# Sixteen modulation pieces moved between three stages, and gate products over the whole array, in a two-block model on one core

## The chip, the cores and the metric

The kernel runs on one core of a Trainium2 chip. The metric is the device time of one execution in microseconds. The kernel before was run three times: median 3736.88 us, lowest 3733.0, highest 3741.73. One more execution was recorded by the hardware profiler; it took 3748.67 us, and its span, the time between the first and the last recorded event, is 3746.9 us. All rows below are from that execution, counted from the span's start.

Five engines work side by side, each through its own list of instructions in order: PE (matrix products), DVE and POOL (elementwise), ACT (functions, copies) and SP, which here only issues DMAs. Nearly all DMAs of the kernel are issued by SP and share one hardware queue.

## The reference, cut to what matters

Two blocks run one after the other on 512 tokens of width 1024, in f32. The change lies in the first. Its layer 0 mixes by Fourier transforms, its layer 1 is an RWKV layer; both end in a mixture of 16 experts.

```python
for i in range(DEPTH):                       # first block, two layers
    sh1x, sc1x, g1x, sh2x, sc2x, g2x = split(silu(c) @ ada_w[i] + ada_b[i], 6)   # modulation, and so for ctx
    hx = rmsnorm(x, norm_g[i, 0]) * (1.0 + sc1x) + sh1x
    if i % 2 == 0: x = x + g1x * fourier_mix(hx, ...)
    else:                                    # RWKV, for x and ctx together 768 rows
        xr, xw, xk, xv, xa, xg = [h + (h_shift - h) * mix[j] for j in range(6)]
        r, k, v = xr @ wr, xk @ wk, xv @ wv
        decay[d] = f(w0[d] + tanh(xw @ w1[d]) @ w2[d])     # low rank, two directions d
        a[d] = sigmoid(a0[d] + (xa @ a1[d]) @ a2[d])       # low rank
        ...                                  # scan over time, output
    hx = rmsnorm(x, norm_g[i, 1]) * (1.0 + sc2x) + sh2x
    x = x + g2x * ec_moe(hx, ...)            # per expert the top 64 tokens (ctx: 32) and their gates
```

The product `silu(c) @ ada_w[1]` makes 6144 numbers for x and as many for ctx. Its first 8 of 24 pieces of 256 columns are made early; the other 16, the late pieces (n from 8 to 23), are needed only after the RWKV layer's projections.

## The kernel before, in words

**The RWKV layer's projections** run in this order on PE. First three low-rank products on mixed inputs (`lps`, L1193), while DVE and POOL make the mixed inputs (`c_mix`, L1085). Then r (eight blocks of 128 output columns, 512 tokens each), then v (eight blocks, 768 tokens), then the keys (eight blocks, 768 tokens). A block of these is made of products `pj` (L929 to L931): each f32 factor is split in a high and a low part, and three products make one. The split weights of a block come through one raw buffer `wraw` (load L913), an ACT cast to `whi` and a subtraction to `wlo` (L893, L894).

**The late modulation pieces** stand in the generator `modulation` (L1110). One piece is two half-pieces; each loads 512 KB (`adw`, L1119) and issues products of 32 columns of the array side by side (`mods`, L1128). After the second half ACT copies the result (`adasb`), and two small products (`mod2`, L1139) turn it. In the kernel before two half-pieces run ahead of the first `lps`, and all the others are placed between the products of r and v, by `beside=mods` in the function `big`, one step for every second index k.

**The key stage.** For each block m, `k_ahead(m)` (L1245) loads its small weights `w2`, `w0` and `a2` and the stored r and v (`rm`, `vm`), makes the decay logits `zps` (L1264), the rates `aps` (L1270) and cumulated decays `cps` (L1277). `k_evac(m)` takes the finished keys, makes their squared norm (`kn`, L1303), its inverse root `rn`, spreads it (`rnb`, L1315), multiplies (`kk`, L1317), and makes the tiles `bkt`, `art` (L1331 to L1339) and the bonus `bon` (L1353) that goes to `vm` (L1354). The tiles go to memory by stores (`keep`, L1283 to L1290), and `vm` by the store at L1356. A scheduler puts the instructions of each engine in order by its own estimates; what is in the code's text one behind the other can stand interleaved in the lists. On SP the order of the loads and stores is fixed by this too.

**The gates of the experts.** For each four experts, q from 0 to 3, `places(q)` makes matrices `Pm` of zeros and ones (L586), and `gates(q)` (L589) multiplies them by stored values to get each chosen token's number and gate. In each it uses products with 64 columns (L595) and, with ctx (layer 0), 32 columns (L599) of the array; DVE copies the sums out (L602 to L605), and a gather by POOL (L610) reads the chosen rows.

## Time and profile before

| what | value |
|---|---|
| median of three runs | 3736.88 us |
| profiled execution, and its span | 3748.67 us, 3746.9 us |
| PE busy | 3497.8 us (93% of the span) |
| DVE, ACT, POOL busy | 1745.7, 1134.1, 548.8 us (47%, 30%, 15%) |
| mean granted TensorE clock | 0.947 of full speed |

A busy time is the union of an engine's instructions. The whole span is dense on PE, so the reader asks for each stretch what PE waits for there, and not which engine is busiest on the whole. The stages in which the change works take 29.2 us (low-rank products), 149.8 us (r and v) and 207.4 us (keys) of the span.

### The profile page before, as it was taken

The numbers are of one execution on the slowest core, as the hardware profiler recorded it, in microseconds if no ns is written. First come the engines' busy times: TensorE is split into PE (matmuls) and PEld (weight loads), VectorE is DVE, ScalarE is ACT, GpSimd is POOL, SyncE is SP. The second block draws the span as 40 slices with busy tenths as digits, with TensorE's granted clock in tenths as the row PEclk, the third lists the DMA queues.
The fourth block names the chain that finished last, engine by engine and source line by source line (L and its number), as shares of the span: only waits on it lengthen the run. The fifth ranks groups of instructions, "written<-read, shape, count | busy, mean of one in ns | idle before, by whom it ended". The sixth has DMA issues, their size and how long they took to land. (4 is left out here: it accounts for less than half of the span.)

```text
span 3746.9 us, 64431 instructions
## 1 busy us (share of the span) xinstructions
PE 3497.8 (93%) x27320; PEld 2202.8 (59%) x27320; DVE 1745.7 (47%) x3279; ACT 1134.1 (30%) x2018; POOL 548.8 (15%) x458
## 2 busy tenths in 40 slices
PE   7989999997998688898999999999999989999999
PEld 4643333334787578886433335656788746567887
DVE  4522223228345578863112127845544558454443
ACT  3211110116446455532000004433322234242222
POOL 3100000002112233311000002220111222201111
PEclk9989999998998779998999998999999979999999
DMA  8489898852846757646999991111333321113332
GB/s 292 169 310 369 344 363 335 342 217 90 243 124 165 168 123 166 141 123 259 380 408 394 393 350 54 35 41 30 104 96 96 93 57 40 36 39 103 97 97 81
DMA packets 585941, 690.21 MB, mean 184 GB/s; under 512 B 178921, under 2 KB 454207, under 8 KB 585142
## 3 DMA queue, kind: packets, MB, share of 16 engines
q1 hardware_dynamic: 574192, 664.44, 52.7%
q10 hardware_dynamic: 8934, 13.12, 1.0%
q0 software_dynamic: 2528, 8.53, 0.6%
q8 instruction: 215, 3.52, 0.4%
q14 instruction: 72, 0.59, 0.0%
HBM read 646.17 MB, written 39.85 MB: 183 GB/s over the span
## 5 line engine op out<-in xcount | busy, mean ns | idle before, releaser
L893 ACT CAST whi<-wraw 128x1024 fp32r<-128x1024 f32 (+3 forms) x236 | 233.3, 989 | 684.7 <-PE pj L930 107.9
L640 PE MATMUL GU<-we,Xe 128*32 128x512 f32 x2048 | 306.0, 601 | 3.4 <-DVE hid L645 3.4
L894 DVE TENSOR_TENSOR wlo<-wraw,whi 128x1024 fp32r<-128x1024 f32 (+3 forms) x196 | 232.1, 1184 | 79.4 <-ACT whi L893 79.3
L665 PE MATMUL Y<-we,hidT 128*32 128x512 f32 x2048 | 262.1, 597 | 5.0 <-DVE Zc L697 3.5
L640 PE MATMUL GU<-we,Xq 128*32 128x512 f32 x2048 | 251.3, 610 | 0.0
L645 DVE TENSOR_TENSOR hid<-hid,GU 64x1536 f32<-64x1536 f32 (+1 forms) x32 | 47.7, 1491 | 360.0 <-ACT hid L644 359.9
L640 PE MATMUL GU<-we,Xc 128*32 128x512 f32 x1024 | 190.0, 597 | 0.0
L644 ACT ACTIVATE hid<-GU 64x1536 f32<-64x1536 f32 (+1 forms) x32 | 39.3, 1229 | 459.4 <-PE GU L640 459.3
L1985 POOL TENSOR_TENSOR u<-u 128x512 f32<-128x512 f32 x64 | 94.2, 1474 | 530.7 <-ACT uph L1984 530.7
L640 PEld LDWEIGHTS GU<-we,Xe 128*32 128x32 f32 x2048 | 79.0, 111 | 151.7 <-issue 145.9
L640 PEld LDWEIGHTS GU<-we,Xq 128*32 128x32 f32 x2048 | 67.6, 113 | 160.2 <-issue 157.7
L929 PE MATMUL pj<-hTh,whi 128*128 128x512 f32 (+1 forms) x352 | 155.5, 442 | 4.1 <-ACT hTh L1015 2.8
L665 PEld LDWEIGHTS Y<-we,hidT 128*32 128x32 f32 x2048 | 70.0, 110 | 148.9 <-issue 145.1
L931 PE MATMUL pj<-hTh,wlo 128*128 128x512 f32 (+1 forms) x352 | 149.6, 425 | 0.0
L930 PE MATMUL pj<-hTl,whi 128*128 128x512 f32 (+1 forms) x352 | 148.8, 423 | 0.0
L894 POOL TENSOR_TENSOR wlo<-wraw,whi 128x1024 fp32r<-128x1024 f32 x40 | 96.1, 2403 | 309.3 <-ACT whi L893 286.5
L654 DVE COPY hidT<-htp 128x512 f32<-128x512 f32 (+1 forms) x48 | 27.6, 600 | 209.7 <-PE htp L653 121.7
L929 PE MATMUL pj<-xh,whi 128*128 128x512 f32 (+1 forms) x320 | 120.6, 377 | 0.4 <-ACT xh L893 0.4
L710 DVE SCALAR_TENSOR_TENSOR xres<-sps,mod,xres 128x512 f32<-128x512 f32 x128 | 89.1, 746 | 64.9 <-PE sps L709 64.3
L930 PE MATMUL pj<-xl,whi 128*128 128x512 f32 (+1 forms) x320 | 115.0, 360 | 0.4 <-DVE xl L894 0.2
L931 PE MATMUL pj<-xh,wlo 128*128 128x512 f32 (+1 forms) x320 | 115.0, 359 | 0.0
L2152 ACT COPY PT<-tp 128x256 f32<-128x256 f32 (+3 forms) x128 | 51.2, 405 | 149.6 <-PE tp L2150 149.4
(2160 smaller groups left out, 7853.0 us busy)
## 6 DMA issues: line engine op xcount, KB each, us to landing
we<-in_moe_wd_dram SPq DMA_DIRECT2D x128, 1024.0 KB
we<-in_moe_wg_dram SPq DMA_DIRECT2D x126, 1024.0 KB
we<-in_moe_wu_dram SPq DMA_DIRECT2D x126, 1024.0 KB
ada<-in_ada_w_dram SPq DMA_DIRECT2D x32, 1024.0 KB
wraw<-in_w_up_dram SPq DMA_DIRECT2D x64, 512.0 KB
wraw<-in_w_down_dram SPq DMA_DIRECT2D x64, 512.0 KB
wraw<-in_w_in_dram SPq DMA_DIRECT2D x42, 512.0 KB
adw<-in_ada_w_dram SPq DMA_DIRECT2D x32, 512.0 KB
```

Of the source, the lines that this page charges most:

```text
L640: nc.tensor.matmul(GU[j:j + 32, g, :], xs[g][:, kk, :], ws[m][:, k, h * 512:(h + 1) * 512], start=kk == 0, stop=kk == 7, tile_position=(0, j))
L644: nc.scalar.activation(hid[up], GU[lo], AF.Silu)
L645: nc.vector.tensor_tensor(hid[up], hid[up], GU[up], ALU.mult)
L665: nc.tensor.matmul(Y[j:j + 32, 0, :], hidT[:, g, k, 32 * kh:32 * kh + 32], w[:, kh, h * 512:(h + 1) * 512], start=kh + k == 0, stop=kh * k ...
L710: nc.vector.scalar_tensor_tensor(r_[:, c, :], ps, g2[:, c, s:s + 1], r_[:, c, :], op0=ALU.mult, op1=ALU.add)
L893: e.nc.scalar.copy(hi, src)
L894: (eng or e.nc.vector).tensor_tensor(lo, src, hi, ALU.subtract)
L929: nc.tensor.matmul(ps, a[0], b[0], start=start, stop=False)
L930: nc.tensor.matmul(ps, a[0], b[1], start=False, stop=False)
L931: nc.tensor.matmul(ps, a[1], b[0], start=False, stop=stop)
L1985: nc.gpsimd.tensor_tensor(u, u, u, ALU.mult)
L2152: nc.scalar.copy(PT[:, :nb], tp[:, :nb])
```

## The change

Three things are changed.

First, the gates: products over the whole array. `Pm` is stored so that two experts' 64 columns, or four experts' 32, lie side by side as one matrix of 128 columns, and each product takes the values of all of them; the sums that belong to other experts are left unread. Per q there are 8 products where there were 16, and with ctx 2 where there were 8. DVE copies out by halves or quarters of the partitions: with ctx 8 copies instead of 4, without ctx 2 instead of 1.

Second, the 16 late pieces. Pieces 8 to 13 stand beside the mixing and the low-rank products, pieces 14 to 23 beside the key products; none stands beside r or v. The ACT copy of a piece is made in two halves.

Third, the buffers of the key stage: `w2` and `a2` have one buffer instead of two, and `sq` and `ks` share one.

```diff
         def gates(q):
-            pz = pm.tile([P, 3, 2], F32, name="pz", tag="m")
-            for i in range(4):
-                o = 64 * (i % 2)
+            pz = pm.tile([P, 3, 4, 2], F32, name="pz", tag="m")
+            es = lambda a, n_: V[:, t, 4 * q + a:4 * q + a + n_, :]
+            for j in range(2):
                 for t in range(4):
-                    nc.tensor.matmul(pz[o:o + 64, i // 2, :], Pm[:, t, i, :], V[:, t, 4 * q + i, :], start=t == 0, stop=t == 3,
-                                     tile_position=(0, o))
...
+                    nc.tensor.matmul(pz[:, j, 0:2, :], Pm[:, t, 2 * j:2 * j + 2, :].rearrange("p a b -> p (a b)"), es(2 * j, 2), start=t == 0, stop=t == 3)
             if with_ctx:
...
+                for t in (4, 5):
+                    nc.tensor.matmul(pz[:, 2], Pc[:, t - 4].rearrange("p a b -> p (a b)"), es(0, 4), start=t == 4, stop=t == 5)
+                for i in range(4):
+                    r = slice(32 * i, 32 * i + 32)
+                    nc.vector.tensor_copy(zc[r, q, :], pz[r, 2, i, :])
+                nc.vector.tensor_copy(ic[:, q:q + 1], zc[:, q, 0:1])
+            for h in range(2):
+                r = slice(64 * h, 64 * h + 64)
+                nc.vector.tensor_copy(zx[r, 2 * q:2 * q + 2, :], pz[r, 0:2, h, :])
+            if with_ctx:
+                nc.vector.tensor_copy(ix[:, 2 * q:2 * q + 2], zx[:, 2 * q:2 * q + 2, 0])
...
-        def modulation(pw):
+        def modulation(pw, ns, tag):
-            todo = [(n, h) for n in range(8, 24) for h in range(2)]
+            todo = [(n, h) for n in ns for h in range(2)]
...
-                    sb = pw.tile([P, 256], F32, name="adasb", tag="adasb")
-                    nc.scalar.copy(sb, ps[:, :256])
-                    yield 1
-                    p2 = pm.tile([P, T], F32, name="mod2", tag="ev")[:, :4].rearrange("p (a b) -> p a b", b=2)
+                    p2 = pm.tile([P, T], F32, name="mod2", tag=tag)[:, :4].rearrange("p (a b) -> p a b", b=2)
                     for b in range(2):
-                        nc.tensor.matmul(p2[:, b, :], sb[:, b * P:(b + 1) * P], e.t("sel2"), start=True, stop=True)
+                        sb = pw.tile([P, P], F32, name="adasb", tag="adasb")
+                        nc.scalar.copy(sb, ps[:, b * P:(b + 1) * P])
+                        yield 1
+                        nc.tensor.matmul(p2[:, b, :], sb, e.t("sel2"), start=True, stop=True)
...
-            mods = modulation(pw)
+            mods = modulation(pw, range(8, 14), "ev")
...
                     c_mix(e, h, x_[:, dt, :], j, dt, n)
+                    next(mods)
...
-            big(e.d["rw_wr"][0], x_, SEGS[:1], r_evac, beside=mods)
+            big(e.d["rw_wr"][0], x_, SEGS[:1], r_evac)
...
-            big(e.d["rw_wv"][0], x_, SEGS, v_evac, beside=mods)
...
-            w2 = pw.tile([65, 2, P], F32, name="w2", tag="w2", bufs=2)
-            a2 = pw.tile([P, P], F32, name="a2", tag="a2", bufs=2)
+            w2 = pw.tile([65, 2, P], F32, name="w2", tag="w2")
+            a2 = pw.tile([P, P], F32, name="a2", tag="a2")
...
-            kt, sq = el("kt", 2), el("sq")
+            kt, sq = el("kt", 2), pw.tile([P, TA], F32, name="sq", tag="kss")
...
-            ks = el("ks", 1, T)
+            ks = pw.tile([P, T], F32, name="ks", tag="kss")
...
-        big(e.d["rw_wk"][0], xk, SEGS, k_evac, k_ahead)
+        mods = modulation(pw, range(14, 24), "mm")
+        next(mods)
+        big(e.d["rw_wk"][0], xk, SEGS, k_evac, k_ahead, mods)
```

On PE, at the start of the low-rank products, stood before two half-pieces and then `lps` alone (a name's number counts tiles and differs between the kernels):

```order
L1128 MATMUL mods_5870<-adw_5676,silu_c_82 32x256 x4
L1128 MATMUL mods_5870<-adw_5678,silu_c_82 32x256 x4
L1193 MATMUL lps_5713<-xf1_5680,lw_5492 128x512
L1193 MATMUL lps_5724<-xf1_5680,lw_5492 128x256
L1193 MATMUL lps_5713<-xf1_5680,lw_5492 128x512 x2
L1193 MATMUL lps_5724<-xf1_5680,lw_5492 128x256
```

At the same place on PE stands now, from the same two half-pieces on:

```order
L1133 MATMUL mods_5646<-adw_5637,silu_c_82 32x256 x4
L1133 MATMUL mods_5646<-adw_5639,silu_c_82 32x256 x4
L1199 MATMUL lps_5711<-xf1_5641,lw_5453 128x512
L1199 MATMUL lps_5722<-xf1_5641,lw_5453 128x256
L1199 MATMUL lps_5711<-xf1_5641,lw_5453 128x512
L1144 MATMUL mod2_5667<-tab_58,adasb_5668 128x2
L1133 MATMUL mods_5687<-adw_5651,silu_c_82 32x256 x4
L1144 MATMUL mod2_5667<-tab_58,adasb_5675 128x2
L1133 MATMUL mods_5687<-adw_5661,silu_c_82 32x256 x4
```

The first `lps` still stand behind the first two half-pieces; the second piece and all later ones stand between `lps`, ten half-pieces up to the first product of r.

On SP, in the key stage, stood before behind the store of block 2's `vm` (`sp_bv`) the loads of block 4's `w2`, `w0` and `a2`:

```order
L1290 DMA sp_ar1_5636<-art_7771 128x4x64
L1356 DMA sp_bv_5633<-vm_7498 128x512
L1250 DMA w2_7900<-in_rw_w2_dram 64x2x128
L1251 DMA w2_7900<-in_rw_w0_dram 1x2x128
L1252 DMA a2_7901<-in_rw_a2_dram 128x128
L1254 DMA rm_7905<-sp_r_5634 128x512
L1255 DMA vm_7906<-sp_bv_5633 128x512
```

On SP, around the same store of block 2, stands now:

```order
L1296 DMA sp_ar1_5597<-art_7670 128x4x64
L1124 DMA adw_7719<-in_ada_w_dram 128x4x256
L1362 DMA sp_bv_5594<-vm_7355 128x512
L1124 DMA adw_7796<-in_ada_w_dram 128x4x256
L918 DMA wraw_7810<-in_rw_wk_dram 128x8x128
L1124 DMA adw_7808<-in_ada_w_dram 128x4x256
L1256 DMA w2_7826<-in_rw_w2_dram 64x2x128
L1257 DMA w2_7826<-in_rw_w0_dram 1x2x128
L1258 DMA a2_7827<-in_rw_a2_dram 128x128
```

Three loads of 512 KB now stand between that store and block 4's `w2`. Behind the store of block 1's `vm` it is two `adw` loads and then block 3's `w2`, behind that of block 3 two `adw` loads and block 5's; behind that of block 0 one `adw` load and the row of block 2's `w0`. Before, blocks 2 and 3 had their `w2` loaded ahead of the first of these stores.

On PE, in the key stage, stood before, in block 4, the cumulated decays together ahead of the next products of the keys:

```order
L1353 MATMUL bon_8034<-ks_7978,k_tabc_5645 128x512
L1277 MATMUL cps_8039<-k_tabc_5645,sg_7909 128x128 x4
L1277 MATMUL cps_8050<-k_tabc_5645,sg_7909 128x128 x2
L1277 MATMUL cps_8058<-k_tabc_5645,sg_7910 128x128 x4
L1277 MATMUL cps_8068<-k_tabc_5645,sg_7910 128x128 x2
L929 MATMUL pj_8094<-xh2_7079,whi_8090 128x512
```

On PE, at the same place of block 4, stands now:

```order
L1359 MATMUL bon_7968<-ks_7910,k_tabc_5606 128x512
L1283 MATMUL cps_7973<-k_tabc_5606,sg_7835 128x128 x4
L1133 MATMUL mods_7980<-adw_7796,silu_c_82 32x256 x4
L934 MATMUL pj_7987<-xh2_6862,whi_7812 128x256
L935 MATMUL pj_7987<-xl2_6863,whi_7812 128x256
L936 MATMUL pj_7987<-xh2_6862,wlo_7813 128x256
L1283 MATMUL cps_7991<-k_tabc_5606,sg_7835 128x128 x2
L934 MATMUL pj_7987<-xh2_6862,whi_7812 128x256
L935 MATMUL pj_7987<-xl2_6863,whi_7812 128x256
L936 MATMUL pj_7987<-xh2_6862,wlo_7813 128x256
L1283 MATMUL cps_7999<-k_tabc_5606,sg_7836 128x128 x4
L1133 MATMUL mods_7980<-adw_7808,silu_c_82 32x256 x4
```

Between the four `cps` groups stand now two half-pieces and three products of the keys at a time.

## Rows read from the trace of the kernel before

**Rows 1.** Windows: length, busy PE, PEld, DVE, ACT, POOL; clock, DMA share, GB/s.
```profile
885.60:914.80 29.20, 29.15 (x80) 16.07 (x81) 27.40 (x45) 21.15 (x39) 8.29 (x5) 0.93 0.12 33
914.80:1064.60 149.80, 148.49 (x928) 110.00 (x927) 64.89 (x92) 66.57 (x110) 18.96 (x11) 1.00 0.70 206
1064.60:1272.00 207.40, 177.18 (x1139) 149.94 (x1137) 116.86 (x136) 132.23 (x224) 56.26 (x44) 0.90 0.60 148
```

**Rows 2.** Timeline of PE, low-rank products; columns: start, us, engine, line, operation.
```profile
885.65 4.81 PE L1193 MATMUL lps<-xf,lw 128*128 128x512 f32 x7 [11.13 <-issue]
```

**Rows 3.** Groups of PE instructions in r and v, 914.8 to 1064.6.
```profile
L1128 PE MATMUL mods<-adw,silu_c 128*32 128x256 f32 x240 | 19.2, 391 | 0.5 <-DMA adw<-in_ada_w_dram 0.4
L1139 PE MATMUL mod<-tab,adasb 128*128 128x2 f32 x64 | 8.4, 236 | 0.1
```

**Rows 4.** Timeline of PE: one half-piece among the products of r.
```profile
923.93 0.39 PE L931 MATMUL pj<-xh,wlo 128*128 128x512 f32 x1
924.25 0.64 PE L1128 MATMUL mods<-adw,silu_c 128*32 128x256 f32 x8
...
925.16 0.39 PE L930 MATMUL pj<-xl,whi 128*128 128x512 f32 x1
925.39 0.39 PE L931 MATMUL pj<-xh,wlo 128*128 128x512 f32 x1
```

**Rows 5.** Timeline of ACT: two successive blocks of v.
```profile
1052.75 0.59 ACT L1216 COPY vt<-pj 128x512 f32<-128x512 f32 x1 [5.05 <-PE pj L931]
1061.73 0.59 ACT L1216 COPY vt<-pj 128x512 f32<-128x512 f32 x1 [5.05 <-PE pj L931]
```

**Rows 6.** Timeline, all engines: a weight block's load, cast and subtraction.
```profile
949.34 0.37 SPq L913 DMA_DIRECT2D wraw<-in_rw_wr_dram  x1
954.65 1.05 ACT L893 CAST whi<-wraw 128x1024 fp32r<-128x1024 f32 x1 [0.68 <-DMA wraw<-in_rw_wr_dram]
955.73 1.23 DVE L894 TENSOR_TENSOR wlo<-wraw,whi 128x1024 fp32r<-128x1024 f32 x1 [1.84 <-ACT whi L893]
...
1024.09 0.39 SPq L913 DMA_DIRECT2D wraw<-in_rw_wv_dram  x1
...
1028.38 1.05 ACT L893 CAST whi<-wraw 128x1024 fp32r<-128x1024 f32 x1 [0.21 <-DMA wraw<-in_rw_wv_dram]
```

**Rows 7.** Waits of PE in the key stage: in total, times, longest.
```profile
PE cps L1277 <- DVE vm L1354: 15.0, 5, 3.1
```

**Rows 8.** Timeline of SP in the key stage: DMA issues.
```profile
1139.49 1.22 SPq L1356 DMA_DIRECT2D sp_bv<-vm  x1
...
1162.20 1.37 SPq L1356 DMA_DIRECT2D sp_bv<-vm  x1
1163.68 0.75 SPq L1250 DMA_DIRECT2D w<-in_rw_w_dram  x1
1164.48 0.64 SPq L1251 DMA_DIRECT2D w<-in_rw_w_dram  x1
```

**Rows 9.** Timeline of PE: rnb of key blocks 1 to 3, zps.
```profile
1118.76 1.53 PE L1315 MATMUL rnb<-tab,rn 128*64 128x128 f32 x24
...
1141.05 1.53 PE L1315 MATMUL rnb<-tab,rn 128*64 128x128 f32 x24
...
1167.15 2.90 PE L1264 MATMUL zps<-w,tw 65*128 65x128 f32 x12 [4.46 <-DMA w<-in_rw_w_dram]
1169.99 2.83 PE L1315 MATMUL rnb<-tab,rn 128*64 128x128 f32 x24
```

**Rows 10.** Timeline of PE: gates with ctx, a 128-column product, gates without ctx.
```profile
580.68 0.63 PE L595 MATMUL pz<-V,Pm 128*64 128x2 f32 x8
...
583.67 0.17 PE L599 MATMUL pz<-V,Pm 128*32 128x2 f32 x1
...
1084.96 1.50 PE L1303 MATMUL kn<-k_tabc,sq 128*128 128x2 f32 x12
...
1766.69 1.41 PE L595 MATMUL pz<-V,Pm 128*64 128x2 f32 x32
```

More of the change, by code (lines that the diff above doesn't have):

```diff
@@ L1125, in modulation @@
                 if h == 0:
-                    ps = pm.tile([P, T], F32, name="mods", tag="ev")
+                    ps = pm.tile([P, T], F32, name="mods", tag=tag)
                 for k in range(4):
@@ L1200, in c_proj @@
                             nc.scalar.activation(tw[d][0:64, c0:c0 + wd], ps[d * 64:d * 64 + 64, :wd], AF.Tanh)
+            for _ in mods:
+                pass
             x_ = mixsplit(px, pw, 0, T)
@@ L1227, in v_evac @@
                     nc.sync.dma_start(sp["v"][:, hh, m, :].rearrange("(t p) n -> p t n", p=P), vn[:, :, hh * 64:hh * 64 + 64])
-            big(e.d["rw_wv"][0], x_, SEGS, v_evac, beside=mods)
-            for _ in mods:
-                pass
+            big(e.d["rw_wv"][0], x_, SEGS, v_evac)
             xk = mixsplit(px, pw, 2, TA)
@@ L1356, in k_evac @@
             nc.sync.dma_start(sp["bv"][:, m, :], vm)
-        big(e.d["rw_wk"][0], xk, SEGS, k_evac, k_ahead)
+        mods = modulation(pw, range(14, 24), "mm")
+        next(mods)
+        big(e.d["rw_wk"][0], xk, SEGS, k_evac, k_ahead, mods)
+        for _ in mods:
+            pass
 def weave(*gens):
```

14 lines of the change are left out of this document (4 added, 10 removed).

## The prediction, made before the change was run

> **What bounds the kernel now.** I read the windows by stage first, since a share over the whole span mixes stages with different limits. In the low-rank stage PE is busy for 29.15 of 29.20 us and the DMA engines for 0.12 of the time; in r and v PE is busy for 148.49 of 149.80 us at a granted clock of 1.00; in the key stage it is busy for 177.18 of 207.40 us only, at a mean clock of 0.90 [rows 1]. So r and v are bound by PE, and what is taken from PE there is gained. The low-rank stage is bound by PE too once it has begun. The key stage is bound by something else, and the question there is what.
>
> The waits of PE in the key stage name `vm`: 15.0 us in five waits of about 3 us before the last `cps` of a block [rows 7]. But the timelines of SP and PE show a longer loop: `rnb` of block m-1, then kk, bkt and art, then that block's stores on SP up to `vm`, then on SP the load of block m+1's `w2`, then `zps` of block m+1, which stands on PE ahead of `rnb` of block m. In one turn it reads: `rnb` at 1141.05, the store of `vm` issued at 1162.20 (21.15 us later), `w2` issued at 1163.68 and its second part at 1164.48, `zps` at 1167.15 after 4.46 us of waiting for it, and `rnb` at 1169.99 [rows 8, 9]: 28.9 us. The turn before it, in which `w2` had been loaded ahead, took from 1118.76 to 1141.05, 22.3 us [rows 9]. The queue of SP thus decides how long a turn is, where the load of `w2` stands behind the stores.
>
> **The change part by part.** *r and v lose their pieces.* The 240 records of `mods` are 30 half-pieces at 8 records, and the 64 of the small products are 16 pieces at 4 [rows 3]. A half-piece lengthens the stream by 925.16 - 923.93 = 1.23 us less two product slots of 0.23 (925.16 to 925.39), so 0.77 us [rows 4]. Without pieces r takes 8 blocks x 8 x 3 products x 0.23 = 44.2 us, and v eight times the period of two undisturbed blocks, 1061.73 - 1052.75 = 8.98, so 71.8 us [rows 4, 5]. That is 116.0 of 149.8, and 33.8 go: 30 x 0.77 = 23.1 for half-pieces, and the rest, 10.7, for 32 small products, 0.33 each.
>
> *What is late next in r* is its weights. Through one raw buffer a block's load, cast and subtraction follow each other: 1024.09 to 1028.38, then 1.05, then 1.23, so 6.6 us [rows 6], against 5.5 of products. The rows don't show how many blocks stand ready when r begins. The bounds are 0 and 8 x 1.1 = 8.8 us; I take 3.7, since the lengthened stage before gives the first blocks time. r and v save 30.1.
>
> *The low-rank stage gains ten half-pieces and twelve small products.* PE stood idle for 11.13 us before its first `lps` [rows 2], and that idle time stays, since the first `lps` still stand ahead of the second piece. After it PE is full, so all count: 10 x 0.77 + 12 x 0.33 = 11.7 us. Were the pieces as short as records back to back, ten at 0.64 [rows 4], it would be 6.4; that is the lower bound. Their loads find DMA engines that are nearly idle [rows 1]. The keys then begin 30.1 - 11.7 = 18.4 us earlier.
>
> *The key stage gains ten pieces*: 20 x 0.77 + 20 x 0.33 = 22.0 us of PE. PE has 207.40 - 177.18 = 30.2 us of idle time there [rows 1], so this alone can be hidden. The loads can't be sure of that. On SP two or three `adw` or `wraw` loads of 512 KB now stand between the store of one block's `vm` and the `w2` of the block after next. The trace of before shows none in that place. The nearest rows: a weight load took 5.3 us (949.34 to 954.65) among `adw` loads and 4.3 without (1024.09 to 1028.38), so one more load ahead is worth 1.0 [rows 6]; by bytes, 148 GB/s at a share of 0.60 is 247 GB/s, and 512 KB take 2.1 us [rows 1]. I take 1.4, nearer to the row that times a load, since at the end of a block's stores the queue is not full: the second part of `w2` was issued by 1165.1 and had landed 2.0 us later [rows 8, 9].
>
> By turns: the start, two half-pieces ahead of the first `zps`, +1.5. Block 2, one load, +1.4. Block 3, whose `w2` was ahead and now stands behind a store and two loads: its turn of 22.3 could become 28.9 + 2.8, +9.4; but part of the 21.15 was itself waiting for the PE order of a denser block, so I take +6. Block 4, three loads, of which the last waits until PE has used the one before: +3, between 0 and 8. Block 5, two loads less what `w2` had to spare: +2. Together +13.9. Against it, products of the keys and half-pieces now stand between the `cps` and fill the waits for `vm`; where the loop isn't bound by the queue, in the last blocks, I credit 3 of the 15.0 us. The key stage becomes 11 us longer, with ends at -18 and +40 (below). One buffer for `w2` and `a2` costs nothing further, since the loads stand behind the stores anyway; one buffer for `sq` and `ks` makes `sq` of a block wait for `bon` of the one before, which stands well ahead of it on PE, and I price it at 0, at most 2.
>
> *The gates.* With ctx a q takes from 580.68 to 583.84, 3.16 us for 48 records; without ctx 32 records take 1.41 [rows 10]. After it there are 20 and 16 records with 128 columns. Twelve such records of another product took 1.50, so 0.125 each [rows 10]: 2.5 and 2.0 us. That is -0.7 four times and +0.6 four times. DVE has four more copies in front of the first gather, some 0.3 us. Sum -0.5, between -4 and +3. The 64-column records take 0.044 us each where they are alone (1.41 / 32), against 0.125 for a 128-column one, so the whole array is no bargain there [rows 10]. The Trainium skill (TensorEngine Tiling (Array Packing), section Key Properties) has a rule that speaks against this part: tiles of a divided array work independently, so that two products of 64 columns can go side by side. By it the whole array would gain nothing in either layer, and the sum below would be 0.4 us less of a gain; the rows of the layer with ctx, 0.066 a record, don't show that parallel work, and I stay with the rows.
>
> *The sum*: -18.4 + 11 - 0.5 = -7.9 us. The profiled execution took 3748.67 us, 11.8 more than the median of the runs; what I worked out is a difference, and I set it against the median: 3736.9 - 7.9 = 3729.
>
> **The rivals.** *PE fills its waits and bounds the key stage.* For it: 30.2 us of idle time against 22.0 of new work, and the interleaved `cps`. Then the key stage keeps its length, the change gains 18.9 us, and the time is 3718. If the denser work also keeps the clock at 1.00, 177.2 us at 0.90 shrink to 159.5, and with 22.0 more the stage could end up to 18 us earlier: 3700. Against it: the loop over SP is not shorter for any of that, and it took 28.9 us in a turn whose PE work is about 20. I take 3716 for this case. The Trainium skill (TensorE: Matmul & The Clock Gate, section HAM oscillation) says that a wait in every turn of a loop brings the clock down in every turn. It speaks for this rival if the waits go, and for the next one if they don't.
>
> *The queue costs more than the pieces gave: slower.* Its place is the stretch on SP between the store of `vm` and `w2`, in blocks 2 to 5. If each load there costs its 2.1 us, the new turn of block 3 its full 9.4 us, and the third load of block 4 another 4 for its own wait, the four turns cost 2.1 + 10.8 + 10.3 + 4.2 = 27.4. And where PE waits, the products behind run at the lower level of its clock, 1.2 GHz: `rnb` took 2.83 us after the wait of 4.46, and 1.53 else [rows 9], `zps` likewise; 2.7 us a turn, 10.8 for four. With the start that makes 40 us. It decides from 18 us on, where what r and v gave is used up. Half way between, at +28, the kernel is 9 us slower, 3746. Against it: the early turns have slack that the price of 9.4 ignores.
>
> *r stays as long as it was*, since its weights come no faster: a block's cycle with `adw` loads among them was 949.34 to 956.96, 7.6 us [rows 6], and eight are 60.8 where I count 47.9. Then the whole comes out 5 us slower than before, 3742. Against it: the cycle held two `adw` loads, and these leave r.
>
> **How the numbers follow.** My forecast has 0.48, PE as the bound 0.25, the queue 0.17, r's weights 0.10. A measurement of this kernel can tell some 0.2%, 7.5 us, from no change. My case, alone from 3722 to 3737, lies on that border, so its 0.48 are 0.26 faster and 0.22 same; PE as the bound is faster but for 0.01; the weights' case is same but for 0.01 slower; the queue's is 0.15 slower and 0.02 same. Together faster 0.50, same 0.34, slower 0.16. The range holds 8 in 10: it begins at 3711, inside the first rival, and ends at 3747, inside the second.
>
> **What would show it.** In the windows after: r and v together at 116 to 124 us, the low-rank stage at 40 to 42, the keys beginning some 18 us earlier, and a key stage of about 218 us. In SP's timeline the `w2` of blocks 3 to 5 issued behind two or three loads, and on PE waits of `zps` for `w` of 2 to 5 us. The forecast is wrong if `zps` doesn't wait there and the key stage is no longer than 207 us, or if r's casts wait for `wraw` in every block.

## The result: slower, 3777 us where 3729 was predicted

The changed kernel took 3777.11 us (median of six runs, 3771.0 to 3781.09), the kernel before on the same chip 3737.99. The ratio is 1.009, with a 95% interval from 1.0075 to 1.0105. The profiled execution took 3771.0 us.

Windows of the changed kernel, cut where the work of the three rows of [rows 1] begins and ends, with r and v apart, and at last the key stage cut from v's last product to the last `rnb` (columns as in [rows 1]):

```profile
875.20:915.85 40.65, 39.83 (x181) 20.56 (x181) 32.98 (x55) 31.11 (x60) 11.56 (x7) 0.95 0.42 130
915.85:968.00 52.15, 46.56 (x200) 35.77 (x196) 27.11 (x33) 28.05 (x47) 7.95 (x4) 1.00 0.35 107
968.00:1044.20 76.20, 72.47 (x430) 62.56 (x431) 30.54 (x38) 28.03 (x45) 7.43 (x4) 1.00 0.49 137
1044.20:1295.60 251.40, 206.71 (x1338) 159.97 (x1337) 116.01 (x147) 133.78 (x241) 57.74 (x44) 0.86 0.64 165
1043.86:1293.21 249.35, 204.67 (x1318) 157.92 (x1317) 114.48 (x145) 134.04 (x241) 57.15 (x43) 0.86 0.63 164
```

Against [rows 1]: the low-rank stage has grown by 11.4 us (29.20 to 40.65), r and v have shrunk by 21.4 (149.80 to 128.35), and the key stage has grown by 44.0 (207.40 to 251.40). The loss is there. (Ahead of the first `lps` the two profiled executions differ by another 10.4 us, 885.65 against 875.24; the last section comes back to it.) The last row's cut is the one used for all kernels below; for the kernel before it reads

```profile
1064.27:1269.51 205.24, 175.02 (x1119) 147.86 (x1117) 116.37 (x135) 132.48 (x224) 53.94 (x40) 0.91 0.60 146
```

so PE has 29.7 us more work (204.67 against 175.02) and 14.5 us more idle time (44.7 against 30.2). Groups of PE instructions in that cut show the work, first of the changed kernel, then of the kernel before:

```profile
L1270 PE MATMUL zps<-w,tw 65*128 65x128 f32 x192 | 32.5, 324 | 7.6 <-DMA w<-in_rw_w_dram 7.6
L1276 PE MATMUL aps<-ta,a 64*128 64x512 f32 (+1 forms) x64 | 21.0, 556 | 0.0
L1133 PE MATMUL mods<-adw,silu_c 128*32 128x256 f32 x160 | 14.6, 440 | 16.1 <-DMA adw<-in_ada_w_dram 16.1
L1144 PE MATMUL mod<-tab,adasb 128*128 128x2 f32 x40 | 6.6, 234 | 0.4 <-ACT adasb L1142 0.4
```

```profile
L1264 PE MATMUL zps<-w,tw 65*128 65x128 f32 x192 | 26.5, 289 | 4.6 <-DMA w<-in_rw_w_dram 4.5
L1270 PE MATMUL aps<-ta,a 64*128 64x512 f32 (+1 forms) x64 | 14.6, 509 | 0.0
```

The pieces' products are 14.6 + 6.6 = 21.2 us, as priced (22.0). The other 8.5 us lie with the old products: a `zps` takes 324 ns where it took 289, and an `aps` 556 where it took 509, at a mean granted clock of 0.86 where it was 0.91. (The busy times of the two groups have grown by 6.0 and 6.4 us. That is also because their products now stand singly between others and overlap less with each other, so these two numbers don't add up to a price of the clock.) The idle time, by the waits of PE from 1045 to 1297 in the changed kernel:

```profile
PE mods L1133 <- DMA adw<-in_ada_w_dram: 16.1, 7, 7.4
PE zps L1270 <- DMA w<-in_rw_w_dram: 7.6, 1, 7.6
PE kn L1309 <- ACT sq L1304: 5.4, 3, 2.1
PE cps L1283 <- DVE vm L1360: 5.0, 3, 2.0
PE pj L934 <- ACT whi L898: 4.3, 1, 4.3
PE rnb L1321 <- DVE rn L1313: 2.8, 1, 2.8
```

The 15.0 us for `vm` [rows 7] have fallen to 5.0, so the pieces did fill waits. But PE now waits 16.1 us for the pieces' own data, 3.1 more for `w`, and 4.3 for a weight block. The longest turn (from one `rnb` to the next) shows where they come from. SP's timeline there:

```profile
1160.83 1.33 SPq L1296 DMA_DIRECT2D sp_ar<-art  x1
1162.26 1.22 SPq L1124 DMA_DIRECT2D adw<-in_ada_w_dram  x1
1163.56 0.61 SPq L1362 DMA_DIRECT2D sp_bv<-vm  x1
1164.27 0.38 SPq L1124 DMA_DIRECT2D adw<-in_ada_w_dram  x1
1164.70 0.67 SPq L918 DMA_DIRECT2D wraw<-in_rw_wk_dram  x1
1169.15 0.37 SPq L1124 DMA_DIRECT2D adw<-in_ada_w_dram  x1
1169.57 0.65 SPq L1256 DMA_DIRECT2D w<-in_rw_w_dram  x1
```

and PE's, from the half-piece ahead of the turn on:

```profile
1140.37 0.64 PE L1133 MATMUL mods<-adw,silu_c 128*32 128x256 f32 x8
...
1159.64 1.01 PE L1309 MATMUL kn<-k_tabc,sq 128*128 128x2 f32 x4 [1.67 <-ACT sq L1304]
1168.01 1.08 PE L1133 MATMUL mods<-adw,silu_c 128*32 128x256 f32 x8 [7.36 <-DMA adw<-in_ada_w_dram]
1173.38 0.79 PE L934 MATMUL pj<-xh,whi 128*128 128x512 f32 x1 [4.29 <-ACT whi L898]
...
1181.76 1.55 PE L1321 MATMUL rnb<-tab,rn 128*64 128x128 f32 x12
```

Read against [rows 8, 9]: the load for the half-piece at 1168.01 goes into the buffer that the half-piece at 1140.37 had read. It went out only at 1162.26, behind the stores, and PE stood until 1168.01. The weights of key block 4 went out at 1164.70 (before, this block's load had gone out at 1079.80), and PE stood again until 1173.38. All that follows up to the next `rnb`, 12 key products among it, ran at a granted clock of 0.50 (windows, 1168.00 to 1181.76; a product of 512 columns took 0.63 us where [rows 4] have 0.39), and the turn took 38.8 us (1142.95 to 1181.76).

Turns of the key stage, from the starts of `rnb` in PE's timeline, and PE's busy time in each (ahead of them, from v's last product to the first `rnb`, 27.8 us before and 36.1 after):

| kernel | seven turns, us |
|---|---|
| before | 26.7, 22.3, 28.9, 26.4, 29.3, 25.0, 18.9 |
| before, PE busy | 21.4, 19.1, 23.6, 23.4, 26.1, 21.8, 12.4 |
| after | 32.3, 30.8, 38.8, 30.5, 34.9, 25.6, 20.5 |
| after, PE busy | 29.2, 29.4, 23.1, 29.1, 23.9, 25.6, 12.9 |

The second turn, before and after, and the third after, as windows:

```profile
1118.76:1141.05 22.29, 19.10 (x132) 15.83 (x132) 13.82 (x17) 16.41 (x28) 7.06 (x5) 1.00 0.53 120
```

```profile
1112.18:1142.95 30.77, 29.36 (x209) 22.55 (x208) 14.54 (x19) 16.32 (x31) 7.37 (x5) 1.00 0.68 176
1142.95:1181.76 38.81, 23.05 (x137) 17.31 (x136) 15.91 (x20) 17.19 (x31) 7.32 (x5) 0.71 0.68 178
```

So two kinds of turn have grown. In turns 1, 2, 4 and 6 PE is nearly full: it idles for 3.0, 1.4, 1.4 and 0.0 us, and the turns are longer, by some 19 us together, because more work stands in them. The second turn has 75 key products where it had 38, besides four half-pieces. In turns 3 and 5 PE idles for 15.8 and 11.0 us, and they are longer by 15.5 us. The third has only 22 key products where it had 67: the list puts most of one block's into the turn before, and the next block's weights come late. The stretch ahead of the first `rnb` adds 8.3 us, half of it in waits of half-pieces for their loads (3.73 and 0.78 us), and the last turn 1.6.

r and v save 21.4 us instead of 30.1. The waits of PE from 910 to 1045, of the changed kernel:

```profile
PE pj L936 <- DVE wlo L899: 3.1, 5, 1.0
PE vtp L1232 <- ACT vc L1226: 2.8, 2, 2.0
PE pj L934 <- ACT whi L898: 2.7, 4, 1.7
```

PE's work is 46.56 + 72.47 = 119.0 us there, and 9.3 us are idle.

### The profile page after: what moved, and what is told of

Its sections match the earlier page's. It is cut to its first block, busy times and chain, and to the rows that moved or that the text cites. A ratio compares the mean times of both kernels' runs of the same rounds, so it can differ in the third digit from the quotient of the medians.

```text
span 3769.1 us, 64068 instructions
## 1 busy us (share of the span) xinstructions
PE 3487.1 (93%) x27144; PEld 2191.9 (58%) x27144; DVE 1744.6 (46%) x3299; ACT 1132.7 (30%) x2031; POOL 548.9 (15%) x458
## 5 line engine op out<-in xcount | busy, mean ns | idle before, releaser
L649 ACT ACTIVATE hid<-GU 64x1536 f32<-64x1536 f32 (+1 forms) x32 | 39.3, 1229 | 450.6 <-PE GU L645 450.6
L659 DVE COPY hidT<-htp 128x512 f32<-128x512 f32 (+1 forms) x48 | 27.7, 599 | 207.4 <-PE htp L658 119.6
```

Of the source, the lines that this page charges most:

```text
L649: nc.scalar.activation(hid[up], GU[lo], AF.Silu)
```

## The experiments

Letters name theories. A: the pieces' loads on SP's queue make the stage long. B: the shared buffers do. D: the order of the lists does. E: the pieces' PE time simply adds. F: the turns get uneven shares of key products. H: two key blocks' weights are loaded late. S: PE's idle time hides nothing. The table has all runs; work and idle time of PE are from the windows between v's last product and the last `rnb`, in the profiled execution. The key stages of before, e1_gates and e2_ten_rv have the same lists of PE and of SP; their 205.2, 202.3 and 200.3 us show how far single profiles of one stage lie apart, 5 us. Smaller differences in that column tell nothing.

| kernel | ratio to before, 95% | stage = work + idle, us | longest turn |
|---|---|---|---|
| before | 1 | 205.2 = 175.0 + 30.2 | 29.3 |
| after | 1.0090 [1.0075, 1.0105] | 249.3 = 204.7 + 44.7 | 38.8 |
| e1_gates | 0.9999 [0.9984, 1.0013] | 202.3 = 171.8 + 30.5 | 29.0 |
| e2_ten_rv | 1.0009 [0.9991, 1.0027] | 200.3 = 169.5 + 30.8 | 29.0 |
| e3_buf | 1.0022 [1.0008, 1.0037] | 208.2 = 173.9 + 34.3 | 33.4 |
| e4_no_loads | 1.0069 [1.0041, 1.0098] | 241.9 = 204.6 + 37.4 | 33.8 |
| g6_noload_oldbuf | 1.0043 [1.0026, 1.0060] | 227.9 = 199.7 + 28.1 | 32.2 |
| x1_loads_only | 1.0046 [1.0026, 1.0067] | 238.9 = 185.8 + 53.1 | 36.3 |
| x3_old_first | 1.0115 [1.0094, 1.0136] | 247.1 = 206.3 + 40.8 | 42.3 |
| x4_double | 1.0068 [1.0046, 1.0089] | 240.8 = 211.0 + 29.8 | 37.4 |
| g2_key_first | 1.0100 [1.0069, 1.0130] | 252.9 = 208.2 + 44.7 | 44.9 |
| e5b_poolq | 1.0060 [1.0036, 1.0083] | 233.6 = 196.9 + 36.7 | 35.0 |
| g4_pool_key_first | 1.0044 [1.0027, 1.0060] | 227.4 = 200.0 + 27.5 | 34.0 |
| z1_even_order | 1.0069 [1.0044, 1.0095] | 247.2 = 208.1 + 39.1 | 42.8 |
| z2_even_pool | 1.0052 [1.0034, 1.0070] | 240.7 = 207.8 + 32.8 | 38.0 |
| z3_before_even | 0.9988 [0.9969, 1.0006] | 206.1 = 180.1 + 26.0 | 28.6 |
| v1_wk_poolq | 1.0059 [1.0038, 1.0080] | 241.6 = 205.2 + 36.3 | 34.9 |
| v6_both_off_sp | 1.0053 [1.0037, 1.0070] | 234.8 = 203.0 + 31.8 | 34.0 |
| c1_late_weights | 1.0011 [0.9996, 1.0027] | 212.2 = 174.8 + 37.4 | 34.8 |
| p1_pool_no_products | 0.9999 [0.9984, 1.0014] | 212.8 = 173.4 + 39.3 | 34.1 |

### Which of the three parts costs time

**e1_gates** is the kernel before with the new gates alone.

> The kernel before with the gate products over the whole array alone. Theory (the loss is in the key stage's queue): the gates cost nothing that shows, -0.5 us as predicted, between -4 and +3; ratio 0.999 to 1.001. Rival (the gates are part of the loss, through the copies ahead of the first gather or the longer products): +5 us or more, ratio above 1.0015.

The gates cost and gain nothing that can be measured. Their products with ctx, of the changed kernel, one q as in the first two of [rows 10]:

```profile
L598 PE MATMUL pz<-V,Pm x16: 168/253/253, 574.5 to 576.1; 128*128 128x4 f32 x16
L601 PE MATMUL pz<-V,Pc x4: 256/256/256, 576.2 to 576.5; 128*128 128x8 f32 x4
```

(durations in ns, least, median and most; first and last start.) That is some 2.3 us for 20 records where 48 took 3.16.

**e2_ten_rv** is the changed kernel with the ten pieces beside r and v instead of the keys, and the key stage's old buffers.

```diff
+            mods = modulation(pw, range(14, 24), "ev")
+            next(mods)
-            big(e.d["rw_wr"][0], x_, SEGS[:1], r_evac)
+            big(e.d["rw_wr"][0], x_, SEGS[:1], r_evac, beside=mods)
```

> The changed kernel with pieces 14 to 23 put back beside r and v and the key stage as before; gates and the six pieces beside the low-rank products stay. Theory (all of the loss is in the key stage): the key stage is 205 to 210 us, r and v some 136 to 141, the low-rank stage 40.5, and the whole -4 to +2 us against before, ratio 0.999 to 1.0005. Rival (the low-rank stage or the gates cost part of the loss): +8 us or more.

The low-rank stage took 40.3 us and r and v 137.9: the six pieces cost 11.1 there and saved 11.9 here. The whole loss thus belongs to the ten pieces beside the keys and the buffers that came with them. With them goes the second half of what r and v saved: 137.9 to 128.4, 9.6 us for ten pieces where six had saved 11.9.

**e3_buf** is the kernel before with the key stage's smaller buffers alone.

```diff
-            w2 = pw.tile([65, 2, P], F32, name="w2", tag="w2", bufs=2)
+            w2 = pw.tile([65, 2, P], F32, name="w2", tag="w2")
-            kt, sq = el("kt", 2), el("sq")
+            kt, sq = el("kt", 2), pw.tile([P, TA], F32, name="sq", tag="kss")
```

> The kernel before with the key stage's buffers of the changed one alone (one buffer for w2 and a2, one shared by sq and ks). Theory A (the loads of the pieces in SP's queue make the loss): the key stage gains 0 to 8 us, since w2 of blocks 2 and 3 now comes behind the stores; ratio 1.000 to 1.002. Rival B (the missing buffers make most of the loss): +20 us or more, ratio above 1.005.

The buffers alone cost 0.2% by the runs; the 3 us in the key stage lie within what single profiles differ by. B doesn't carry 44.

### Loads or products

**e4_no_loads** is the changed kernel in which the keys' pieces all read the first half-piece's data, so that their other 19 loads go and their products stay. **g6_noload_oldbuf** is that with the old buffers.

```diff
+                    if one and i:
+                        ws[i] = ws[0]
+                        return
```

> The changed kernel with the loads of pieces 14 to 23 left out but for one: all their products read that one tile, so the products, copies and places on PE stay and 19 loads of 512 KB go. It leaves out that data of the pieces. Theory A (loads in SP's queue): the waits of mods for adw (16.1 us) and most of zps for w2 go, the key stage is 205 to 220 us and the whole 30 to 45 us less than the changed kernel, ratio to before 0.996 to 1.001. Rival B (buffers) or C (the products of pieces and keys placed between zps and rnb): the key stage stays above 235 us, ratio above 1.005.

> The kernel without the loads of pieces 14 to 23 (all their products read one tile, so it leaves out that data), with the key stage's buffers as before the change (two for w2 and a2, sq and ks apart). The order on PE still has zps ahead of the products in five blocks, in three of them behind a store's w2. Theory B (the missing buffers make zps wait): the key stage falls from 253 to 205 to 220 us, ratio under 1.000. Theory D (order): where w2 is loaded ahead nothing waits, so blocks 1 to 3 get back their 22 to 27 us, the later ones stay at 31 to 34; the stage is 225 to 240, ratio 1.002 to 1.004.

Without the loads 242 us are left, where A expected 205 to 220, and 228 with the old buffers as well, in the 225 to 240 of D. So A is not all, and beside the pieces the old buffers, with the other list that comes with them, are worth 14 us. In g6_noload_oldbuf PE works for 24.7 us more than before, and the stage is 22.7 us longer: nearly all of the added work lies on the path.

**x1_loads_only** leaves the products of the keys' pieces out and keeps their loads.

> The changed kernel with the products and copies of pieces 14 to 23 left out: their loads stay in SP's queue, and DVE copies two columns of each so that its buffer comes free (the pieces' values are not computed). Buffers as in the changed kernel. From the first key product to the last rnb: 202 us in the kernels with the key stage of before, 249 in the changed one, 208 with the buffers alone. Theory E (the pieces' time on PE comes in full, since the loop gives PE no free time where they stand): 212 to 225 us here, the pieces' 22 and more being gone; ratio 1.001 to 1.004. Rival A (the loads make the loss): 238 or more, ratio above 1.005.

It has 239 us, just inside the range of A. Products alone cost 23 (g6_noload_oldbuf), loads and buffers 34, buffers 3, and all together 44: the parts don't add, so each changes something that the others change too. The waits of PE in x1_loads_only show one such thing (before it was 4.5 us in one wait):

```profile
PE zps L1277 <- DMA w<-in_rw_w_dram: 29.5, 4, 10.3
```

**x3_old_first** is g6_noload_oldbuf with the next block's key products traced ahead of `zps` and `rnb`; **x4_double** is x3_old_first with each product of the keys' pieces made twice.

```diff
-                        step()
+                        if ahead is None or m < 2 or (c0 == 0 and k < 2):
+                            step()
```

> Pieces 14 to 23 as products only (one tile for all, their data left out), the key stage's buffers as before, and the key products traced ahead of zps and rnb. Neither loads nor buffers nor products in the loop are left, only the pieces' own work on PE, 22 us by the durations of before. Theory E: the stretch is 220 to 230 us against 202, ratio 1.002 to 1.005. Theory D (order): under 212, ratio under 1.001.

> The last kernel with each product of pieces 14 to 23 made twice: 20 more groups of 0.64 us on PE and nothing else. Theory E (PE's time comes in full): 10 to 14 us more than the last kernel. Rival (PE has idle time that takes them): under 4 us more.

x3_old_first fits neither theory. The order made it worse (228 to 247 us), and twice the products made it better (241, with 9.4 us more of `mods`). More work can't shorten the stage by itself; what else differs is the list, which the scheduler makes anew for each kernel. The work grew by 4.7 us, and the idle time fell from 40.8 to 29.8.

### Queues and order

**g2_key_first** is the changed kernel with the edit of x3_old_first. **e5b_poolq** is the changed kernel with the loads of the keys' pieces on POOL's queue. **g4_pool_key_first** has both edits.

```diff
-        mods = modulation(pw, range(14, 24), "mm")
+        mods = modulation(pw, range(14, 24), "mm", nc.gpsimd)
```

> The changed kernel with one edit: from block 2 on, the steps that make zps and rnb are traced behind the block's key products, so that on PE the products stand ahead of the zps that waits for w2, and not between zps and rnb. Pieces, their loads in SP's queue and the buffers stay. Theory D (order: PE stops at zps with the products behind it, and these then run inside the loop): the key stage falls from 252 to 215 to 230 us, the whole 20 to 35 us below the changed kernel, ratio to before 1.000 to 1.004. Rival A (the loads in SP's queue): the stage stays above 240 us, ratio 1.006 or more. Rival B (the buffers): above 240 too.

> The changed kernel with the loads of pieces 14 to 23 issued by POOL on its own queue, and no edit of the order. Its list on PE is that of the kernel without loads. Theory D (order): the key stage stays at 240 to 255 us, ratio 1.005 to 1.009. Rival A (the loads in SP's queue): it falls under 225, ratio under 1.002. The run without loads speaks for D.

> The same edit of the order, and the loads of pieces 14 to 23 issued by POOL on its own queue and not by SP. Theory D with a part for the loads: the key stage falls to 205 to 222 us, the whole to between 18 us faster and 4 us slower than before, ratio 0.995 to 1.001. Rival A alone: it falls as far below the run with the order alone as that run stayed above 240. Rival B (buffers): stays 15 to 20 us above the 203 to 208 of the kernel before.

The order alone gives nothing (D falls as a cure). The loads off SP's queue give 16 us (233.6, between the ranges of A and D), and with the order 22 (227.4, above the 205 to 222 that was expected).

e5b_poolq also tells what the loads cost as such. It has the list of SP of e4_no_loads, and the same list of PE but for two records of `mods` near its start; 19 loads of 512 KB more go out beside it, on POOL's queue. It isn't longer (233.6 against 241.9 us, ratios of 1.0060 and 1.0069). On that list, then, it is not the bytes that cost time; the loads' place in SP's queue and the lists themselves are left.

The waits of PE in g4_pool_key_first from 1048 to 1276:

```profile
PE cps L1284 <- DVE vm L1361: 19.2, 6, 3.5
PE kn L1310 <- ACT Pi L1286: 2.5, 2, 2.2
PE zps L1271 <- DMA w<-in_rw_w_dram: 1.9, 1, 1.9
```

No wait for `adw` or `whi` is left, that for `vm` is back above its old 15.0, and its idle time, 27.5 us, is that of the kernel before, less 2.7. Yet its stage is 22 us longer than before.

**z1_even_order** is the changed kernel with what follows in a key block queued on PE behind the block's last key product, from block 2 on; **z2_even_pool** is that with the pieces' loads on POOL's queue, and **z3_before_even** the kernel before with the same order.

```diff
+                if ahead is not None and m >= 2:
+                    with tc.issue_after(lastpj.ins):
+                        while late:
+                            step()
```

> The changed kernel whole, all loads on SP's queue as they are there; only the order on PE differs: from block 2 of the keys on, what follows rnb's and zps's tracing is issued behind the block's last key product, so that every turn (rnb to rnb) holds 36 key products, or nearly, and all of them stand ahead of the zps that waits for w2. Theory F (uneven turns: a turn costs the longer of the loop and its own PE work, and products behind a waiting zps run at half clock): turns 2 to 5 at 25 to 29 us, the first at 33 since it holds 59 products and six half-pieces, last product of v to last rnb 225 us (217 to 233) against 249 in the changed kernel and 205 before, ratio 1.001 to 1.004. Theory A (the loads between the store of vm and w2 on SP make the turns long): turns 2 to 5 stay at 30 to 39, 243 to 252 us, ratio 1.007 to 1.010. Theory G (start and sharing of DMA engines by loads alone): no change against the changed kernel either.

> As z1_even_order, and the loads of the keys' ten pieces on POOL's queue instead of SP's. Theory F: little more to gain, 1 to 5 us below z1_even_order, so 215 to 230 us from v's last product to the last rnb and a ratio of 1.000 to 1.004. Theory A: most of the gain comes here, 215 to 225 us, while z1_even_order stays at 243 or more. If both stand above 240 us neither theory holds.

> The kernel before with the same forced order in its key stage (40, then 36 products in every turn). A control: the order itself is meant to cost nothing. All theories: 200 to 210 us, turns of 22 to 29, ratio 0.998 to 1.002. If it is slower by over 5 us, the forced order has a price of its own that must be taken off z1_even_order and z2_even_pool.

F falls: z1_even_order had even shares and was no shorter (247 us; turns 38.1, 28.1, 27.5, 42.8, 30.8, 23.3, 20.5). The second, third and fifth turn are shorter than in the changed kernel, and one of 42.8 us stands out. z2_even_pool, at 240.7 us, stayed above 240 too, so that by its expectation neither A nor F holds; z3_before_even, at 206.1, shows that the order alone costs nothing. SP's timeline in the turn of 42.8 us of z1_even_order:

```profile
1198.69 1.29 SPq L1369 DMA_DIRECT2D sp_bv<-vm  x1
1200.04 0.43 SPq L918 DMA_DIRECT2D wraw<-in_rw_wk_dram  x1
1200.56 0.70 SPq L1263 DMA_DIRECT2D w<-in_rw_w_dram  x1
```

and PE's:

```profile
1205.93 0.80 PE L934 MATMUL pj<-xh,whi 128*128 128x512 f32 x1 [9.18 <-ACT whi L898]
```

The weights of the next key block go out behind the store of `vm`, 5.9 us before their first product. This is theory H. It fits the earlier runs: of before, e3_buf, g4_pool_key_first, x4_double and z3_before_even, which have no load of this kind less than 12 us ahead of its first product, only x4_double's doubled pieces give a turn above 34.1; the changed kernel has two (8.7 and 6.5 us ahead), in its turns of 38.8 and 34.9. In all ten kernels with such a load (after, z1_even_order, e4_no_loads, g6_noload_oldbuf, x1_loads_only, x3_old_first, g2_key_first, e5b_poolq, z2_even_pool and below c1_late_weights; 5.9 to 8.7 us ahead) the longest turn is one in which its first product stands. That is a pattern, and not yet a price.

### The late weights, and what is left

**v1_wk_poolq** is the changed kernel with the key weights' loads on POOL's queue. **v6_both_off_sp** has the pieces' loads on POOL's and the key weights' on ACT's. **c1_late_weights** is the kernel before with two weight loads put behind the stores of `vm`.

```diff
+                if ahead is not None and m in (4, 6):
+                    with tc.issue_after(e.vst):
+                        wt = wload(e, w, m * P, P)
```

> The changed kernel with one edit: the loads of the key weights (wraw of rw_wk) go out on POOL's queue instead of SP's, so none of them can stand behind the store of vm. The pieces' loads and the buffers stay. Theory H (late weights): in the changed kernel the weights of blocks 4 and 6 were issued 1.1 and 1.3 us behind a store of vm and their first product came 8.7 and 6.5 us later, in the turns of 38.8 and 34.9 us; here every block's weights are issued at least 12 us ahead of its first product, no turn is above 33, and from v's last product to the last rnb it takes 225 to 235 us against 249 (205 before), ratio 1.002 to 1.006. Theory A (the pieces' loads ahead of w2): two turns of 34 to 39 stay, 242 to 252 us, ratio 1.007 to 1.011.

> The changed kernel with the loads of the keys' pieces on POOL's queue and those of the key weights on ACT's. With the pieces' loads alone on POOL's queue it took 233.6 us, with two late weight loads (6.4 and 6.5 us ahead of their first product) in turns of 35.0 and 31.3. Theory H: no late weights, five turns of 45 products or fewer at 27 to 33, 218 to 230 us, ratio 1.000 to 1.004. If the weight loads have nothing to do with it, 230 to 238 and 1.005 to 1.007, as with the pieces' loads alone.

> The kernel before, no pieces and no change of buffers in its key stage; only the weight loads of key blocks 4 and 6 are put behind the store of vm of blocks 2 and 4 on SP's queue, where the changed kernel has them. Theory H: the turns in which they fall become 32 to 36 us instead of 26 to 29, with PE waiting 4 to 9 us for whi, and 205 us become 214 to 225, ratio 1.002 to 1.005. If late weights don't matter, 203 to 208 and a ratio of 0.998 to 1.002.

In c1_late_weights the load of block 4's weights stands on SP where the changed kernel has it:

```profile
1164.93 1.35 SPq L1360 DMA_DIRECT2D sp_bv<-vm  x1
1166.33 0.80 SPq L913 DMA_DIRECT2D wraw<-in_rw_wk_dram  x1
1167.22 0.81 SPq L1254 DMA_DIRECT2D w<-in_rw_w_dram  x1
```

and PE, with no product left to do, waits at `zps`:

```profile
1172.56 0.77 PE L1268 MATMUL zps<-w,tw 65*128 65x128 f32 x2 [10.27 <-DMA w<-in_rw_w_dram]
...
1178.86 1.53 PE L1319 MATMUL rnb<-tab,rn 128*64 128x128 f32 x24
```

Its two turns are 34.8 and 33.0 us, as expected. But PE waits there for `w` (18.9 us in all), whose load now stands behind the weights', and not for `whi`, so late weights and a late `w2` aren't told apart. The turns behind them are 21.2 each (26.4 and 25.0 before), so that the stage grows by 7.0 us only, to 212.2 where 214 to 225 were expected, and the time by 0.1%, less than the interval can tell. v1_wk_poolq gains 7.8 us (249.3 to 241.6), outside the 225 to 235 that H expected; two of its turns, 34.0 and 34.9 us, are above the 33 of H, though no weights are late, and PE still waits 16.7 us for `adw`. v6_both_off_sp, with the two late loads of e5b_poolq gone, did no better than it: 234.8 against 233.6 us, in the range expected if the weights don't matter. So late weights mark the longest turns, but their price in the stage is 7 to 8 us in two pairs and nothing in the third, hardly more than what single profiles differ by. In v6_both_off_sp PE is nearly full: its first five turns are 28.7, 33.4, 29.8, 34.0 and 29.2, in which PE works for 27.6, 31.1, 27.7, 29.0 and 26.2.

**p1_pool_no_products** is g4_pool_key_first with the PE products of the keys' pieces left out; their loads stay.

```diff
+                if bare:
+                    nc.vector.tensor_copy(e.mod[1][:, 2 * n + h, 0:2], ws[i][:, 0, 0:2])
+                    del ws[i]
+                    load(i + ADB)
```

> As g4_pool_key_first (the keys' pieces' loads on POOL's queue, the next block's key products traced ahead), but the PE products of the ten pieces beside the keys are left out; their loads stay, and a small DVE copy reads each. Theory S (sum): PE's idle time in the key stage is made of waits at fixed places and does not shrink below some 26 to 31 us, so that PE's work adds to the stage in full; g4_pool_key_first took 200.0 us of work and 27.5 of idle, before 175.0 and 30.2. Then this kernel has 174 to 180 us of work, 26 to 32 of idle, 202 to 211 from v's last product to the last rnb against 227, and a ratio of 0.996 to 1.000. Rival: the loads cost the 22 us (sharing the DMA engines, POOL's time to issue them) and the idle could have hidden the products: 218 to 230 us, ratio 1.001 to 1.005.

The windows of g4_pool_key_first and of p1_pool_no_products:

```profile
1047.17:1274.62 227.45, 199.97 (x1318) 156.48 (x1317) 112.93 (x142) 133.06 (x241) 67.43 (x58) 0.90 0.66 173
```

```profile
1045.60:1258.39 212.79, 173.44 (x1119) 146.20 (x1117) 114.61 (x152) 130.62 (x223) 69.84 (x58) 0.91 0.70 185
```

The products' 26.5 us of work went, the stage became 14.7 us shorter, and the idle time grew from 27.5 to 39.3. So S was too strong for this pair: of PE's work on the pieces 15 us lie on the path and 12 are hidden, where g6_noload_oldbuf against the kernel before has 23 of 25 on the path. Its list has one turn without any key product and one with two blocks' (24.9 and 34.1 us), so that part of the 39.3 may be its own: it has the list of SP of e3_buf and nearly its list of PE, and there 34.3 us are idle.

The three steps from before to after then read, in the key stage: loads on POOL's queue, buffers and order +7.6 (p1_pool_no_products), the products +14.7 (g4_pool_key_first), the pieces' loads on SP's queue with the list as the change has it +21.9 (after). The ratios go the same way, 0.9999, 1.0044 and 1.0090, with intervals that don't overlap. The last step goes with the waits that only the changed kernel has of the two, 16.1 us for `adw` and 4.3 for `whi` (idle time in all 17.2 us more, since that for `vm` is shorter). How much of it is due to the loads' place on SP and how much to the list that the scheduler makes around them isn't told apart: no run had the changed kernel's own lists with the loads elsewhere. Of the changes tried none beats the kernel before.

## Why the prediction was wrong

*The low-rank stage* was priced at 29.2 + 11.7 = 40.9 us and took 40.65. Right, in the sum and in its steps: the first `lps` still waits (11.12 us, against 11.13), and what comes behind it is all paid for.

*r and v* were to take 116.0 + 3.7 and took 128.35. The stream without pieces was nearly right (119.0 us of work for the 116.0), the term of what is late next was too small: 5.6 us of idle in r (52.15 - 46.56), inside the bound of 8.8 but above the 3.7 taken, and 3.7 in v (76.20 - 72.47), where none was priced. e2_ten_rv shows where it begins: the first six pieces saved 11.9 us (12.7 by the price of 33.8 for 16), the other ten 9.6 (21.1 by that price).

*The key stage* is the step that failed: 11 us were forecast and 44.0 came. "PE has 207.40 - 177.18 = 30.2 us of idle time there, so this alone can be hidden" was wrong by 15 us (p1_pool_no_products) to 23 (g6_noload_oldbuf), and "Together +13.9" for the loads, with 3 to be credited, was too small: the loads on SP's queue, with the list made around them, cost 21.9 against g4_pool_key_first. Behind the first stands a sum over the stage set against a sum of idle time: the idle time is made of waits of 1 to 5 us at fixed places of each turn (3.0 to 5.4 us a turn in the first six), and a half-piece fills one only where it stands right ahead of the wait on PE's list. The turn of 28.9 us, said to hold "about 20" of PE's work, held 23.56. In g4_pool_key_first the waits for `vm` were 19.2 us with all pieces there. Behind the second stands a list of what is late that had `w2` alone. Nor was it counted that the new list could put the key products of two blocks in one turn and few in the next (75 and 22). The waits for `w` grew by 3.1 us only. I had not counted that a half-piece on PE waits for its own load, 16.1 us in all, and that everything behind it on the list stands with it (in the longest of these waits, 7.36 us, the next key products had no weights either); nor that the loads, and the scheduler's new list, move the loads of the key weights behind the stores. Of block 4's weights the order showed it: the load stands in the rows that were printed of SP, and it was counted there as bytes ahead of `w2`, not as a load that PE waits for.

*The gates* were priced at -0.5 us, between -4 and +3; nothing can be measured, as it should be. The terms of that sum make -0.1 and not -0.5: -0.7 and +0.6, four times each, give -0.4, and the copies add 0.3. The terms themselves hold: 16 records of the whole array took 1.84 us at a clock of 1.00, 0.115 each for the 0.125, and without ctx 16 records took 1.95 us where 32 had taken 1.41.

*The rivals.* That PE fills its waits and bounds the stage happened in turns 1, 2, 4 and 6, but without the gain: more work came into them than they had idle time. r didn't stay as long as it was: it took 52.15 us, and that rival had 60.8. That the queue costs more than r and v gave did, and from further up than its end of +40 us; but its place was not the one named: not `w2` and `zps`, but `adw` and `whi`, for 20.4 of PE's waits. The clock behind the waits, which it priced at 2.7 us a turn, is there: the mean fell from 0.91 to 0.86, and the old products took 8.5 us longer. Not all of it is the clock: g4_pool_key_first, at 0.90, has 25.0 us more work than before, some 4 more than the pieces' own 21.2. I had seen this mechanism and given it 0.17, since the early turns "have slack". The first turn grew by 5.6 us and the second by 8.5, and there it was PE's work that filled them, not the queue. So two causes add up in the key stage, of which this rival had one. The Trainium skill (TensorE: Matmul & The Clock Gate, section HAM oscillation), drawn on for both rivals, says that waits in the turns of a loop bring the clock down in them. In the changed kernel the trace agrees: the granted clock is 0.71 and 0.77 in turns 3 and 5, with 15.8 and 11.0 us of idle time, and 1.00 and 0.98 in turns 2 and 4, with 1.4. But the fifth turn before has 0.77 too, with 3.2 us idle.

*Signs named beforehand.* The keys began 20.4 us earlier (18 were named), but that is luck: 10.4 of them lie ahead of the first `lps`, where only the gates' -0.5 was priced, and the stages that were priced gave 10.0 (21.4 - 11.4). The low-rank stage took what was named, r and v together 128.35 us instead of 116 to 124; the key stage of "about 218 us" was 251. Waits of `zps` for `w` of 2 to 5 us in three blocks didn't come; one of 7.6 did.

## What to carry to other kernels

Idle time of an in-order engine can't be set against new work as a sum: count, wait by wait, what will stand on its list just ahead of each, and take new work as added where nothing does (here 15 of 27 us in one pair of kernels, 23 of 25 in another). A load put into a queue behind stores must be followed to every reader, its own first, and the loads that it pushes back, weights above all, to theirs; and where a scheduler makes the lists, a part taken out alone changes the lists too, so that single parts don't add up to the whole.

## What was not expected of the chip

The stretch ahead of the first `lps`, in which the change alters only the gates of the mixture of experts there, differs by up to 9 us between profiled executions of kernels that are alike there: the first `lps` began between 878.70 and 885.65 us in the four kernels with the old gates (mean 883.1) and between 872.05 and 880.92 in the sixteen with the new ones (mean 876.6). The means are 6 us apart, more than the 0.5 us priced for the gates. Four gates with ctx lie in that stretch, and from first to last record their products took 15.4 us in all before and 11.4 after; whether the rest is theirs stays open, since e1_gates shows no gain beyond its interval (0.16%, 6 us). A difference of that size between two single profiles is thus read stage by stage, and not from their spans (3769.1 and 3746.9, 22.2 apart, where the medians are 39 apart).
